# Projections spread over the attention chunks of an mLSTM layer, and the decay exponents in tiles of their own

## The chip, the cores and the metric

The kernel runs on one core of a Trainium2 chip. The metric is the device time of one execution in microseconds, median of several runs. The engines are named as in the profile: PE (TensorE, matrix products, with PEld its weight loads), DVE (VectorE), ACT (ScalarE), POOL (GpSimd) and SP, which issues the DMAs. Every engine runs its own queue in order and waits for the others at semaphores.

## The reference, cut to what matters

Two layers over 1024 latent and 256 context tokens of width 1024, in fp32. Layer 0 mixes with a short convolution, layer 1 with a bidirectional mLSTM; each is followed by a squared-ReLU MLP, which is most of the work. The change lies in the mLSTM mixer. Per direction, head and chunk of 128 tokens it computes

```python
b = jnp.cumsum(fc, axis=-1)
logd = b[..., :, None] - b[..., None, :] + ic[..., None, :]
logd = jnp.where(tri, logd, -jnp.inf)
inter = b + m[..., None]
m_t = jnp.maximum(inter, jnp.max(logd, axis=-1))
s = jnp.einsum('bhtd,bhsd->bhts', qc, kc) * jnp.exp(logd - m_t[..., None])
w_inter = jnp.exp(inter - m_t)
num = jnp.einsum('bhts,bhsv->bhtv', s, vc) + w_inter[..., None] * jnp.einsum('bhtd,bhdv->bhtv', qc, c_mat)
den = jnp.sum(s, axis=-1) + w_inter * jnp.einsum('bhtd,bhd->bht', qc, n_vec)
out = num / jnp.maximum(jnp.abs(den), jnp.exp(-m_t))[..., None]
...
c_new = a[..., None, None] * c_mat + jnp.einsum('bhsd,bhsv->bhdv', kc * wk[..., None], vc)
```

The outputs of both directions are added, normalized per head, multiplied with `sigmoid(o)` and projected with `w_out`. There are 8 heads with keys of 64 and values of 128.

## The kernel before, in words

**Precision.** A fp32 operand of a large product is split into a high and a low part in a PE format (`load_w`: DMA into `raw`, ACT casts the high part, DVE subtracts for the low part); a product then takes three passes. `raw` has three buffers, and the parts lie in a ring of eight slots, so that four weights are alive at a time. The small products of the attention are fp32 in one instruction, which shows as two records.

**The stage.** It works on head pairs j = 0 to 3. `Pair.k`, `.v` and `.q` project keys (three groups of tokens, `psk`), values (ten tiles, `psv`) and queries (two groups, `psq`) of a pair, each into one of the two PSUM tiles of the pool `tp`, from where ACT copies them to `kT`, `V` and `qz`. A gate stage on DVE and ACT (scans over all tokens, exponents) makes the rows of decays, of which `wkcol`, `acol` and `flcol` are transposes by PE (`ptg`), and the rows of maxima and of weights that go to DRAM (`nm_d`, `w_d`).

**States.** `states` goes through the ten chunks: PE transposes the keys (`pk`), DVE multiplies with the decays (`kk`), PE multiplies with the values, ACT and DVE copy the two directions into `sts`; then, for each head, eight dependent scans (L1004) accumulate the chunk states. One of the two directions runs backwards, so the second scan needs the last chunk.

**Attention.** `attend` takes one head, eight chunks. `front(c)`: for each two chunks a DMA broadcasts the rows of maxima to the tile `Dm` (two buffers); DVE adds the mask in place, ACT takes the exponent in place, PE computes keys by queries into `po` (pool `acc`, six PSUM tiles shared with `pk` and `pth`), and DVE multiplies both to `pm`. `back(c)`: four products with `V` and `sts` into the same `po`; ACT takes the absolute value of the denominators (`dn`), DVE maximum and reciprocal, ACT scales one direction (`h`), DVE adds the other (`hb`), ACT squares for the norm. `front` runs one chunk ahead of `back`.

**Gate and read-out.** `out_gate` normalizes `hb` (POOL computes `rstd`), projects the head's gate (two groups of 512, `pso`) and takes the sigmoid into `sg`; `read_out` transposes `hb` (`pth`) and multiplies. Heads 0 to 5 go to DRAM (`gd`), heads 6 and 7 stay in `sg` for the output projection (`op`).

**Order.** The program is written in the order: projections of pair j, gates and read-outs of pair j-1, states of pair j, attention of its two heads. The framework's scheduler then sets a fixed order for each engine at build time, by program order as priority and by what it thinks is ready; so parts of a later projection already stand between the products of the attention. The gates of the last three pairs are kept back to be mixed with the states and the attention of the last pair and to stand behind it.

Of the kernel before, what the change touches and what calls it, by code (L numbers as in the profile page):

```python
# [8 lines left out]
F32 = mybir.dt.float32  # L9
# [28 lines left out]
def hybrid_kernel(  # L38
# [769 lines left out]
    with ExitStack() as s1:  # L808
# [34 lines left out]
        class Pair:  # L843
# [12 lines left out]
            def k(self, groups, ps_pool=tp, tag="tp"):  # L856
                for t0, n in groups:
                    ps = ps_pool.tile([P, 512], F32, tag=tag, name="psk")
                    mm_feat(ps[:, 0:n], self.w, t0, n)
                    nc.scalar.copy(self.kT[:, t0 : t0 + n], ps[:, 0:n])  # L860

            def v(self, tiles):
                for t in tiles:
# [14 lines left out]
            def q(self, groups):  # L878
                w = load_w(wq[self.j])
                for t0, n in groups:  # L880
                    ps = tp.tile([P, 512], F32, tag="tp", name="psq")
                    mm_feat(ps[:, 0:n], w, t0, n)
# [4 lines left out]

        XG = ((256, 512), (768, 512))
        pair = Pair(0)
        pair.k(PG[0:2], acc, "acc")  # L890
        pair.v([0, 1, 2, 3, 4, 5, 7, 9])
        for f in pend:
            f(acc, "acc")
        pair.v([6, 8])
        gate_rows()
        pair.k(PG[2:])
        sT.close()
        with pool("gates", bufs=1, side="right") as gp:
# [60 lines left out]
            pair.q(XG)  # L959
            nxt = Pair(1)  # L960
            nxt.k(GROUPS)
# [18 lines left out]
        def states(pair):  # L980
            j = pair.j
            for c in range(NT):
# [9 lines left out]
                sb = 1 - c if c < NCT else NT + 1 - c  # L992
                for hh in range(2):
# [14 lines left out]
        def attend(pair, hh):  # L1008
            h = 2 * pair.j + hh
            kT, V, st = pair.kT, pair.V, sts[hh]  # L1010
            qw = hp.tile([P, SEQ], F32, tag="qw", name="qw")
            for d, r in enumerate((lower, upper)):
                nc.sync.dma_start(qw[r], w_d[d, h].partition_broadcast(64))
                nc.vector.tensor_mul(qw[r], qw[r], qz[hh * 64 : hh * 64 + 64, hh])
            if pair.j < HEADS // 2 - 1:
                hb = hp.tile([P, 8, P], F32, tag="hb", name="hb")
            else:
                hb = pr.tile([P, 8, P], F32, tag="V" if hh else "kT", name="hb")
            ssq = small.tile([P, 8], F32, tag="ssq", name="ssq", bufs=4)
            Dm = {}  # L1020

            def front(c):

                if c % 2 == 0:
                    D2 = hp.tile([P, 2, 2 * P], F32, tag="Dm", name="Dm")
                    nc.sync.dma_start(D2, nm_d[:, h, c * P : (c + 2) * P].partition_broadcast(P))
                    for d in range(2):
                        nc.vector.tensor_add(
                            ch(D2[:, d]), ch(D2[:, d]), mask[:, d].unsqueeze(1).broadcast_to([P, 2, P])
                        )  # L1030
                    Dm[c], Dm[c + 1] = D2[:, :, 0:P], D2[:, :, P : 2 * P]
                Dc = Dm[c]
                for d in range(2):
# [4 lines left out]
                    po[:, 0:P], kT[:, g * P : (g + 1) * P], qz[:, hh, c * P : (c + 1) * P], start=True, stop=True  # L1038
                )
                pm = hp.tile([P, 2, P], F32, tag="pm", name="pm")  # L1040
                nc.vector.tensor_mul(pm, po[:, 0:P].unsqueeze(1).broadcast_to([P, 2, P]), Dc)
                return po, pm

            def back(c, po, pm):
# [3 lines left out]
                for d in range(2):  # L1048
                    nc.tensor.matmul(o[:, d], pm[:, d], V[:, g, hh], start=True, stop=False)
                    nc.tensor.matmul(  # L1050
                        o[:, d], qw[:, c * P : (c + 1) * P], st[:, steps[d], d], start=False, stop=True
# [3 lines left out]
                nc.vector.tensor_max(dn, dn, flcol[:, c, :, h])  # L1055
# [3 lines left out]
                nc.vector.scalar_tensor_tensor(hb[:, c], o[:, 1, 0:P], dn[:, 1:2], h1, ALU.mult, ALU.add)  # L1059
# [155 lines left out]
```

## Time and profile before

| | us |
|---|---|
| median of three runs | 2564.34 (2563.26 to 2567.96) |
| the profiled execution, its own time | 2567.07 |
| its span, first to last instruction | 2565.3 |
| PE busy | 2485.2 (97%) |
| DVE busy | 1649.5 (64%) |
| ACT busy | 1141.6 (45%) |
| mLSTM stage, from the first key projection to the last read-out transpose | 1337.8 to 1809.2 |

The profile names an instruction by line, engine, operation and tile, and says of idle time which engine's instruction ended it. PE's clock has two levels, 1.2 and 2.4 GHz; the granted clock of a stretch is given as a share of the full one. Ends of matmuls are modelled, so starts are the safer reading.

### The profile page before, as it was taken

The page shows a single profiled execution, that of the slowest core. Times are in us where ns is not written, and L with a number is a line of the kernel's source. Part 1 is how long each engine was busy: PE and PEld are TensorE (multiplying, and loading weights), DVE is VectorE, ACT ScalarE, POOL GpSimd, SP SyncE. Part 2 cuts the span into 40 slices and gives each one's busy share as a digit, 9 for nine tenths or more (in the row PEclk, how much of TensorE's full clock was granted, in tenths as well). Part 3 has the DMA queues.
Part 4 walks back from the last instruction along what each step waited for, and adds up shares of the span by engine and source line. Part 5 has one row for each costly group of instructions (what it writes and reads, how often), then busy time and mean ns, then how long its engine had stood idle before and what let it go on. Part 6 is the DMA issues. An engine that isn't in the chain of part 4 may idle for free.

```text
span 2565.3 us, 38800 instructions
## 1 busy us (share of the span) xinstructions
PE 2485.2 (97%) x14520; PEld 2194.7 (86%) x14520; DVE 1649.5 (64%) x3058; ACT 1141.6 (45%) x2503; POOL 107.0 (4%) x229
## 2 busy tenths in 40 slices
PE   8999999999999999999999899999999999999998
PEld 6888887899999998888779788887789999988886
DVE  5777885687676654445864745537479788754565
ACT  6311112565445444334654434345456555544443
POOL 1000000100000000000121100000010000000010
PEclk9999999999999999999999899999999999999999
DMA  8456663436676675555751322222336788676665
GB/s 296 133 175 190 207 191 115 137 133 232 224 258 240 226 247 173 166 169 166 239 182 45 76 76 58 66 67 89 104 121 215 261 268 281 230 253 189 184 225 185
DMA packets 230207, 454.87 MB, mean 177 GB/s; under 512 B 17802, under 2 KB 109242, under 8 KB 230018
## 3 DMA queue, kind: packets, MB, share of 16 engines
q1 hardware_dynamic: 230018, 452.38, 54.5%
q8 instruction: 114, 1.87, 0.3%
q14 instruction: 75, 0.61, 0.1%
HBM read 326.78 MB, written 125.33 MB: 176 GB/s over the span
## 4 chain that ended last, share of the span: by engine, by line
PE 51%; issue 30%; DVE 7%; DMA 7%; ACT 3%; POOL 2%; DVEq 0%; SPq 0%; POOLq 0%; ACTq 0%
PE psd L538 11%; PE op L371 5%; PE psZ L433 4%; PE psW L433 4%; PE psX L433 4%; PE psv L867 3%; PE pso L129 3%; DMA Dm<-nm_d 3%; PE psc L129 3%; PE psb L129 2%; PE psu L129 2%; DMA mraw<-in_mod_w_dram 2%; PE psY L433 2%; PE psq L129 1%; DVE macc L220 1%
## 5 line engine op out<-in xcount | busy, mean ns | idle before, releaser
L538 PE MATMUL psd<-w,hp 128*128 128x512 f32 x3024 | 706.7, 395 | 0.6 <-DVE p L558 0.6
L538 PEld LDWEIGHTS psd<-w,hp 128*128 128x128 f32 x3024 | 568.1, 188 | 135.4 <-DVE p L558 1.5
L533 DVE TENSOR_TENSOR hp<-hr,hp 128x512 fp32r<-128x512 f32 (+1 forms) x226 | 169.0, 750 | 245.3 <-ACT hp L532 244.8
L123 DVE TENSOR_TENSOR w<-raw,w 128x512 fp32r<-128x512 f32 x394 | 267.6, 684 | 61.0 <-ACT w L122 60.6
L122 ACT CAST w<-raw 128x512 fp32r<-128x512 f32 x394 | 242.6, 618 | 119.4 <-DMA raw<-in_w_dram 43.1
L532 ACT CAST hp<-hr 128x512 fp32r<-128x512 f32 (+1 forms) x226 | 151.0, 669 | 312.6 <-PE psd L538 270.6
L433 PE MATMUL psX<-A,w 128*128 128x256 f32 (+1 forms) x1536 | 229.7, 297 | 2.9 <-ACT st L448 2.5
L433 PE MATMUL psZ<-A,w 128*128 128x256 f32 (+1 forms) x1536 | 227.7, 296 | 1.7 <-DVE st L452 1.6
L433 PE MATMUL psW<-A,w 128*128 128x256 f32 (+1 forms) x1536 | 227.1, 296 | 0.0
L433 PEld LDWEIGHTS psX<-A,w 128*128 128x128 f32 x1536 | 212.5, 188 | 4.7 <-ACT st L448 3.6
L433 PEld LDWEIGHTS psZ<-A,w 128*128 128x128 f32 x1536 | 212.2, 188 | 3.1 <-DVE st L452 2.8
L433 PEld LDWEIGHTS psW<-A,w 128*128 128x128 f32 x1536 | 212.1, 188 | 0.2 <-DVE st L454 0.2
L371 PE MATMUL op<-w,zs 128*128 128x512 f32 x864 | 206.1, 398 | 6.3 <-ACT zs L365 4.4
L371 PEld LDWEIGHTS op<-w,zs 128*128 128x128 f32 x864 | 162.8, 190 | 43.3 <-ACT zs L365 5.4
L463 ACT ACTIVATE st<-st 128x256 f32<-128x256 f32 (+1 forms) x192 | 85.1, 444 | 199.0 <-DVE st L454 132.8
L220 DVE SCALAR_TENSOR_TENSOR macc<-mraw,sil,macc 128x1024 f32<-128x1024 f32 x112 | 140.5, 1280 | 37.9 <-DMA mraw<-in_mod_w_dram 37.6
L109 ACT CAST w<-raw 128x1024 fp32r<-128x1024 f32 (+1 forms) x73 | 75.5, 1040 | 162.0 <-PE psc L129 60.0
L110 DVE TENSOR_TENSOR w<-raw,w 128x1024 fp32r<-128x1024 f32 (+1 forms) x73 | 87.6, 1209 | 80.1 <-ACT w L109 79.8
L867 PE MATMUL psv<-w,hT 128*128 128x256 f32 (+1 forms) x960 | 135.2, 295 | 0.5 <-ACT V L874 0.5
L867 PEld LDWEIGHTS psv<-w,hT 128*128 128x128 f32 x960 | 125.3, 194 | 1.1 <-ACT V L874 0.9
L433 PE MATMUL psY<-A,w 128*128 128x256 f32 (+1 forms) x768 | 116.6, 298 | 0.1
L129 PE MATMUL psc<-hT,w 128*128 128x512 f32 (+1 forms) x576 | 113.7, 348 | 0.5 <-DVE hT L279 0.4
(242 smaller groups left out, 3443.7 us busy)
## 6 DMA issues: line engine op xcount, KB each, us to landing
hid_d<-st SPq DMA_DIRECT2D x48, 896.0 KB, 5.0
mraw<-in_mod_w_dram SPq DMA_DIRECT2D x80, 512.0 KB, 4.1
raw<-in_w_dram SPq DMA_DIRECT2D x68, 512.0 KB, 4.2
hr<-hid_d SPq DMA_DIRECT2D x104, 320.0 KB, 3.4
rw<-in_w_dram SPq DMA_DIRECT2D x64, 512.0 KB, 6.0
raw<-t_d SPq DMA_DIRECT2D x128, 256.0 KB, 3.2
hr<-hid_d SPq DMA_DIRECT2D x122, 256.0 KB, 2.9
raw<-in_w_dram SPq DMA_DIRECT2D x96, 256.0 KB, 3.8
```

The costliest lines, as they stand in the source:

```text
L110: nc.vector.tensor_sub(w[1], src, w[0].bitcast(F32))
L122: nc.scalar.copy(w[:, 0], src)
L123: nc.vector.tensor_sub(w[:, 1], src, w[:, 0].bitcast(F32))
L129: nc.tensor.matmul(ps, w[a][:, k * P : (k + 1) * P], hold["hT"][:, k, b, t0 : t0 + n], start=(k == 0 and i == 0), stop=(k == KD - 1 and i ...
L220: nc.vector.scalar_tensor_tensor(ac[v], raw, s, ac[v], ALU.mult, ALU.add)
L371: nc.tensor.matmul(ps[h], zs[:, a, k, :], ws[k][b][:, h * 512 : (h + 1) * 512], start=(k == 0 and i == 0), stop=(k == KD - 1 and i == 2),)
L433: nc.tensor.matmul(ps, w[i][:, a, k * P : (k + 1) * P], A[:, PIECE[i], b, k, :], start=(first and k == 0 and j == 0), stop=(k == 3 and j = ...
L463: nc.scalar.activation(c, c, AF.Relu)
L532: nc.scalar.copy(h[:, 0], r)
L533: nc.vector.tensor_sub(h[:, 1], r, h[:, 0].bitcast(F32))
L538: nc.tensor.matmul(ps, h[:, a, o : o + P], w[:, b], start=(first and j == 0), stop=(last and j == 2))
L867: nc.tensor.matmul(ps[:, 0 : self.g], hold["hT"][:, k, a_, t * P : (t + 1) * P], self.wv[k // self.per][b_][:, k % self.per * self.g : (k ...
```

## The change

Three things, all in the mLSTM stage.

1. The projections return lists of units instead of running. A unit is one group of keys (256 or 512 tokens), one value tile, one group of queries, or half of the products of one 512-token group of a gate (`OutGate`, four units a head). `Spread` gives such a list out evenly over a number of steps. `states` calls it once a chunk (ten steps) and `attend`, which now takes both heads of a pair as one list of 16 chunks, once a chunk between `front(i+1)` and `back(i)`. In the states of pair j (from the second on) stand the gates and read-outs of pair j-1, in its attention the key, value and query projections of pair j+1. For the first pair three value tiles of the second stand in the states, the rest and the queries in the attention. In the last pair's attention stand head 5's gate and read-out, head 6's, and the first half of head 7's gate; the other half and head 7's read-out come behind it. Head 0's gate is projected in the gate stage.
2. The rows of maxima come for one chunk into a tile `row` (three buffers), fetched three chunks ahead; DVE's add of the mask writes `pm` (three buffers), in which the exponent and the product are then done in place. `Dm` is gone.
3. The multiplications of `qw` with the queries are done for both heads of a pair ahead of its attention; their transfers are issued ahead of the states.

```diff
+            def units(self):
+                if self.done:
+                    return []
+                self.done = True
+                return [lambda i=i: self.unit(i) for i in range(4)]
+
+            def unit(self, i):
+                if i == 0:
+                    self.w = load_w(wo[self.h])
+                    self.sg = sgp.tile([P, SEQ], F32, tag="sg", name="sg")
+                if i % 2 == 0:
+                    self.ps = tp.tile([P, 512], F32, tag="tp", name="pso")
...
+            def __call__(self):
+                self.i += 1
+                while self.done * self.steps < self.i * self.n and self.done < self.n:
+                    self.units[self.done]()
+                    self.done += 1
+
...
-            nxt.k(GROUPS)
+            run(nxt.k(GROUPS))
+            gates = [OutGate(h) for h in range(HEADS)]
+            run(gates[0].units())
             for src, dst, c0 in ((wkr, wkcol, 0), (a, acol, NCT), (m, flcol, NCT)):
...
+            def fetch(self, c):
+                row = hp.tile([P, 2, P], F32, tag="row", name="row", bufs=3)
+                nc.sync.dma_start(row, nm_d[:, self.h, c * P : (c + 1) * P].partition_broadcast(P))
+                self.rows[c] = row
+
+            def front(self, c):
+
+                h = self.h
+                Dc = hp.tile([P, 2, P], F32, tag="pm", name="pm", bufs=3)
+                nc.vector.tensor_add(Dc, self.rows[c], mask)
                 for d in range(2):
                     nc.scalar.activation(Dc[:, d], Dc[:, d], AF.Exp, bias=acol[:, c, d, h : h + 1])
...
+        def attend(pair, heads, step):
+            items = [(h, c) for h in heads for c in range(8)]
+            for h in heads:
+                h.begin()
+            nxt_ = heads[0].front(0)
+            for i, (hd, c) in enumerate(items):
+                cur = nxt_
+                if i + 3 < len(items):
+                    items[i + 3][0].fetch(items[i + 3][1])
+                if i + 1 < len(items):
+                    nxt_ = items[i + 1][0].front(items[i + 1][1])
+                step()
+                hd.back(c, *cur)
+
+        NPR = HEADS // 2
+        rest = lambda heads: [u for hd in heads for u in hd.out_gate() + [hd.read_out]]
+        heads, old = [], []
+        for j in range(NPR):
+            old = heads
             if j:
...
+            heads = [Head(pair, hh) for hh in range(2)]
+            for c in range(3):
+                heads[0].fetch(c)
+            if j == 0:
+                units = nxt.v(all_tiles) + nxt.q()
+                states(pair, Spread(units[0:3], NT))
+                units = units[3:]
+            else:
+                states(pair, Spread(rest(old if j < NPR - 1 else old[0:1]), NT))
+                if j < NPR - 1:
+                    nxt = Pair(j + 1)
+                    units = nxt.k(GROUPS) + nxt.v(all_tiles) + nxt.q()
+            last = []
+            if j == NPR - 1:
+                last = heads[1].out_gate()
+                units = rest(old[1:2]) + rest(heads[0:1]) + last[0:2]
+            attend(pair, heads, Spread(units, 16))
+        run(last[2:])
+        heads[1].read_out()
```

The built order of the instructions shows three of the places.

DVE at the end of the gate stage, before: the last row of the gate rows, the low halves of the weights of the second pair's queries (`w_13707`) and head 0's gate (`w_13772`), the transposed decays, then the first pair's states (`kk`, `st`).

```order
L952 TENSOR_SCALAR M__12747<-M__12747 40x1280
L110 TENSOR_TENSOR w_13707<-raw,w_13706 128x1024
L970 COPY wkcol<-ptg 128x10x8 x2
L970 COPY acol<-ptg 128x8x8 x2
L970 COPY flcol<-ptg 128x8x8 x2
L110 TENSOR_TENSOR w_13772<-raw,w_13771 128x1024
L987 TENSOR_TENSOR kk<-pk,wkcol 128x128 x4
L1000 COPY st_12978<-pk 64x129 x2
```

The same place after; `w_12942` is the low half of head 0's gate weight, `w_13720` that of the second pair's queries.

```order
L1008 TENSOR_SCALAR M__12747<-M__12747 40x1280
L110 TENSOR_TENSOR w_12942<-raw,w_12941 128x1024
L110 TENSOR_TENSOR w_13720<-raw,w_13719 128x1024
L1028 COPY wkcol<-ptg 128x10x8 x2
L1028 COPY acol<-ptg 128x8x8 x2
L1028 COPY flcol<-ptg 128x8x8 x2
L1045 TENSOR_TENSOR kk<-pk,wkcol 128x128 x2
L110 TENSOR_TENSOR w_14084<-raw,w_14083 128x1024
L1078 TENSOR_TENSOR qw<-qw,qz 64x1024
```

The gate's weight is now wanted by PE ahead of the transposes, and its subtraction stands where the queries' stood, behind the last of the gate rows; a multiplication of `qw` has come between the first `kk`.

DVE in the attention of the second pair, before: the add of the mask to two chunks of `Dm`, and the rest of three chunks mixed with the normalization of the head before (`hb<-hb,rstd`).

```order
L1028 TENSOR_TENSOR Dm<-Dm,mask 128x256 x2
L1059 SCALAR_TENSOR_TENSOR hb<-po,dn,h_14264 128x128
L1055 TENSOR_TENSOR dn<-dn,flcol 128x2
L1072 TENSOR_TENSOR hb<-hb,rstd 128x512
L1056 RECIPROCAL dn<-dn 128x2
L1041 TENSOR_TENSOR pm<-po,Dm 128x256
```

After, one chunk of the same pair; this row of five repeats, chunk by chunk.

```order
L1094 TENSOR_TENSOR pm<-row,mask 128x256
L1117 TENSOR_TENSOR dn<-dn,flcol 128x2
L1103 TENSOR_TENSOR pm<-po,pm 128x256
L1118 RECIPROCAL dn<-dn 128x2
L1121 SCALAR_TENSOR_TENSOR hb<-po,dn,h_14292 128x128
```

The add no longer comes in twos on a tile that holds two chunks' exponents, but once a chunk, from a tile that nothing else uses.

ACT in the attention of the last pair, before: a sigmoid of a gate among the exponents, with a load of the function table ahead of it and one behind.

```order
L1080 ACT_TABLE_LOAD
L1080 ACTIVATE sg<-pso 128x512
L1058 ACTIVATE h_16107<-po,dn 128x128
L1054 ACTIVATE dn<-po 128x2 x2
L1034 ACT_TABLE_LOAD
L1034 ACTIVATE Dm<-Dm,acol 128x128
```

After, one of five such places in that attention.

```order
L1122 ACTIVATE h_16234,ssq<-hb 128x128
L930 ACT_TABLE_LOAD
L930 ACTIVATE sg<-pso 128x512
L1116 ACTIVATE dn<-po 128x2
L1096 ACT_TABLE_LOAD
L1096 ACTIVATE pm<-pm,acol 128x128
L1120 ACTIVATE h_16268<-po,dn 128x128
```

The shape of the place is the same; what has moved is how often it comes, as three gates of the last pair's time now lie in its attention at even distances.

## Rows read from the trace of the kernel before

**Rows 1.** The page's engines: busy us (share of the span), instructions.

```profile
PE 2485.2 (97%) x14520; PEld 2194.7 (86%) x14520; DVE 1649.5 (64%) x3058; ACT 1141.6 (45%) x2503; POOL 107.0 (4%) x229
```

**Rows 2.** PE's waits, 1380 to 1900 us: for whom, us, times, longest.

```profile
PE po L1037 <- DVE hb L1059: 14.1, 11, 2.1
PE po L1049 <- DVE pm L1041: 8.0, 5, 3.0
PE ptg L965 <- ACT l L947: 4.7, 1, 4.7
PE op L371 <- ACT zs L365: 2.7, 1, 2.7
PE pth L1087 <- DVE hb L1059: 2.1, 1, 2.1
PE op L371 <- DVE zs L366: 1.9, 1, 1.9
PE po L1037 <- DVE dn L1055: 1.8, 1, 1.8
```

**Rows 3.** Windows: length, busy PE, PEld, DVE, ACT, POOL (instructions), PE clock, DMA.

```profile
1555.00:1588.00 33.00, 26.65 (x212) 25.00 (x212) 18.49 (x69) 21.98 (x95) 2.90 (x5) 1.00 0.40 98
1588.00:1640.00 52.00, 52.00 (x302) 45.51 (x302) 12.30 (x12) 12.37 (x20) 0.93 (x1) 1.00 0.17 51
```

**Rows 4.** Windows of 10 us, first and last of five below full clock.

```profile
1460.00:1470.00 10.00, 7.43 (x47) 6.89 (x45) 4.33 (x17) 5.01 (x22) 1.22 (x2) 0.83 0.53 109
...
1680.00:1690.00 10.00, 7.76 (x63) 7.35 (x62) 6.37 (x25) 6.33 (x29) 1.73 (x2) 0.97 0.41 120
```

**Rows 5.** DVE's timeline (start, us, operation, idle before); tile `Dm`: releasers, landing.

```profile
1674.53 0.76 DVE L1028 TENSOR_TENSOR Dm<-Dm,mask 128x256 f32<-128x256 f32 x2 [2.44 <-DMA Dm<-nm_d]
...
  DMA Dm<-nm_d: 39.0, 22
...
DMA to landing us min/median/max: 5.2/5.2/5.2
```

**Rows 6.** PE's timeline: values, two chunk products, gate projections.

```profile
1587.80 17.36 PE L867 MATMUL psv<-w,hT 128*128 128x256 f32 x144 [0.20 <-ACT V L874]
...
1670.08 0.39 PE L1050 MATMUL po<-st,qw 128*128 128x129 f32 x2
1670.31 0.39 PE L1049 MATMUL po<-V,pm 128*128 128x129 f32 x2
...
1785.30 22.19 PE L129 MATMUL pso<-hT,w 128*128 128x512 f32 x94
```

**Rows 7.** Timeline of all engines at the end of the gate stage.

```profile
1418.26 0.56 ACT L860 COPY kT<-psk 128x512 f32<-128x512 f32 x1
...
1418.40 1.29 PE L965 MATMUL ptg<-ident,l 40*128 40x40 f32 x10 [4.66 <-ACT l L947]
1418.42 1.21 DVE L110 TENSOR_TENSOR w<-raw,w 128x1024 fp32r<-128x1024 f32 x1
```

**Rows 8.** DVE's timeline at the end of the second pair's states.

```profile
1546.38 4.86 DVE L1004 SCALAR_TENSOR_TENSOR st<-st,adb 128x258 f32<-128x258 f32 x12
```

**Rows 9.** ACT's table loads: groups (count, busy us, mean ns); timeline of one.

```profile
L1080 ACT ACT_TABLE_LOAD x6 | 7.7, 1283 | 0.1
...
L1034 ACT ACT_TABLE_LOAD x5 | 6.4, 1283 | 2.8 <-DMA Dm<-nm_d 2.7
...
1757.83 1.28 ACT L1034 ACT_TABLE_LOAD   x1
1759.12 0.40 ACT L1034 ACTIVATE Dm<-Dm,acol 128x128 f32<-128x128 f32 x1
```

**Rows 10.** Timelines of PE and DVE at the end of the first pair.

```profile
1484.81 0.64 PE L1050 MATMUL po<-st,qw 128*128 128x129 f32 x2
...
1489.71 1.29 DVE L1072 TENSOR_TENSOR hb<-hb,rstd 128x512 f32<-128x512 f32 x2 [0.86 <-POOL rstd L242]
```

More of the change, by code (lines that the diff above doesn't have):

```diff
@@ L856, in k, with unit @@
             def k(self, groups, ps_pool=tp, tag="tp"):
-                for t0, n in groups:
+                def unit(t0, n):
                     ps = ps_pool.tile([P, 512], F32, tag=tag, name="psk")
@@ L860, in k, with unit @@
                     nc.scalar.copy(self.kT[:, t0 : t0 + n], ps[:, 0:n])
+                return [lambda g=g: unit(*g) for g in groups]
             def v(self, tiles):
-                for t in tiles:
+                def unit(t):
                     ps = tp.tile([P, 512], F32, tag="tp", name="psv")
@@ L958, in hybrid_kernel @@
             ring["n"] += 2
-            pair.q(XG)
+            run(pair.q())
             nxt = Pair(1)
-            nxt.k(GROUPS)
+            run(nxt.k(GROUPS))
+            gates = [OutGate(h) for h in range(HEADS)]
+            run(gates[0].units())
             for src, dst, c0 in ((wkr, wkcol, 0), (a, acol, NCT), (m, flcol, NCT)):
@@ L978, in hybrid_kernel, with states @@
             nc.gpsimd.memset(t[lower, :, 1], 0.0)
-        def states(pair):
+        def states(pair, step):
             j = pair.j
@@ L1006, in states @@
                     )
[L1008 to L1032, printed above, removed]
@@ new lines, in hybrid_kernel, with __init__, begin @@
+        class Head:
+            def __init__(self, pair, hh):
+                self.pair, self.hh, self.h = pair, hh, 2 * pair.j + hh
+                self.qw = hp.tile([P, SEQ], F32, tag="qw", name="qw")
+                for d, r in enumerate((lower, upper)):
+                    nc.sync.dma_start(self.qw[r], w_d[d, self.h].partition_broadcast(64))
+                self.rows, self.gate = {}, gates[self.h]
+            def begin(self):
+                pair, hh = self.pair, self.hh
+                for r in (lower, upper):
+                    nc.vector.tensor_mul(self.qw[r], self.qw[r], qz[hh * 64 : hh * 64 + 64, hh])
+                if pair.j < HEADS // 2 - 1:
+                    self.hb = hp.tile([P, 8, P], F32, tag="hb", name="hb")
+                else:
+                    self.hb = pr.tile([P, 8, P], F32, tag="V" if hh else "kT", name="hb")
+                self.ssq = small.tile([P, 8], F32, tag="ssq", name="ssq", bufs=4)
+            def fetch(self, c):
[6 more added lines that the diff above has]
+                nc.vector.tensor_add(Dc, self.rows[c], mask)
```

106 lines of the change are left out of this document (52 added, 54 removed).

## The prediction, before the changed kernel ran

> **What bounds the kernel now.** I read the page's engine table first: TensorE (PE) is busy 97% of the span [rows 1]. So time can only be won where PE stands still or runs at its half clock, and the change touches only the mLSTM stage, some 1380 to 1810 us. Next the waits of PE in that stage [rows 2]: 26.0 us are in the attention of the four head pairs (14.1 + 8.0 + 2.1 + 1.8, behind `hb`, `pm`, `hb` again and `dn`), 4.7 us behind the gate rows, 4.6 us where the output projection starts. The windows [rows 3] say why the first group can go: in 1555 to 1588, attention of the second pair, PE is busy 26.65 of 33 us and ACT 21.98; in the 52 us behind it, where the rest of the value, the query and the gate projections run, PE is full and DVE and ACT do 12 us each. The work that could fill the holes stands directly behind them. Then the clock [rows 4]: in five slices of 10 us it is under 1, from 0.83 in 1460 to 1470 to 0.97 in 1680 to 1690, each at or behind a PE wait (0.83, 0.83, 0.66, 0.86, 0.97). A slice at clock c loses 10(1 - c) us; the five lose 8.5 us, of which some 1.6 lie inside the 3 us wait that is counted already. So 6.9 us.
>
> What makes PE wait is DVE's queue [rows 5]. The add of the mask is done in place on `Dm`, which holds two chunks and has two buffers; its refill can only be issued when both chunks' products are done, takes 5.2 us to land, and DVE then stands 2.4 us at a time, 39.0 us in 22 waits, with `hb` and `pm` of the chunks before queued behind.
>
> **What goes.** The rows of maxima get a tile of their own, freed by the add itself, one chunk each, three buffers, fetched three chunks ahead; the exponent lies in `pm`. A fetch has three chunks' time instead of less than one transfer. A unit of value projection is 24 of the 144 matmuls in 17.36 us, 2.9 us; a 512-wide unit is 24 of 94 in 22.19, 5.7 us, a gate unit half of that; a chunk's own five fp32 products are 1.1 us, from two starts 0.22 us apart [rows 6]. So a chunk takes 4.0 us or more in pairs two and three, some 2.55 us in the first (two chunks to a unit), about 2.5 to 3.2 in the last. Three chunks are 7.5 to 12 us against 5.2 us for a transfer that is now half as large. I take the DMA wait at zero. And with a unit ahead of each chunk PE has other work while ACT and DVE go through exp, product, maximum, reciprocal. PE's matmuls are the same in number and shape. Removed: 26.0 + 6.9 = 32.9 us, if nothing takes their place.
>
> **What is added**, term by term:
> - The gate stage. Gate 0's projection is put between the keys and the transposes `ptg`. It doesn't cover the 4.7 us wait: its PSUM tile is freed by the copy of keys that ACT runs behind the exponent, at 1418.26 + 0.56, and its third pass wants the low half of the weight, which DVE's order puts behind the whole chain, 1418.42 + 1.21 [rows 7]. PE starts at 1419.6 instead of 1418.4: **+1.2 us** (0 to 2.5). The 11.3 us of gate work are moved, not added; behind them on PE wait `ptg` and with it DVE's `wkcol`, so DVE begins its part of the states later.
> - The scans. Behind the last `pk` of a pair DVE has a copy and 13 more scans, 4.86 us for 12 [rows 8], together some 5.6 us, before the products that read the last state. In the first pair of before 40 value matmuls, 4.8 us, stand there, and PE did not wait. In the changed order I count 15 value matmuls and six products in the first pair, 3.1 us, 20 wide matmuls and three products in the second, 5.3, 17 narrow and 11 wide ones and four products in the third, 5.4, 17 wide ones and four products in the last, 4.8: short by 2.5 + 0.3 + 0.2 + 0.8 = 3.8 us; with some half clock behind the first gap **+4.5 us** (0 to 8).
> - The first pair's states. Two more multiplications of `qw` come ahead of the scans on DVE, each about as long as a subtraction of as many columns, 1.21 us [rows 7], while of PE's value matmuls only 120 stand there (14.4 us) to hide them. Between none of it on the path and all of it with a wait for each of the two, **+2 us** (0 to 4).
> - The first pair's chunks at 2.55 us: nearest is the attention of the second pair in before, 33 us for 14 chunks with its DMA waits [rows 3], 2.36 us. Just enough; **+1.5 us** (0 to 4).
> - The last pair. Its 16 chunks get 12 gate units, and each 512 columns end in a sigmoid among exponents. ACT loads its function table 21 times in the stage instead of 11 (6 + 5), 1283 ns each [rows 9]: 12.8 us more in all, hidden in pairs one to three, where ACT has room. In the last pair's attention: 16 chunks at 1.57 us (21.98 us for 14, [rows 3]) 25.1, ten loads 12.8, five sigmoids, each taken as a copy of 512 columns, 0.56 [rows 7], 2.8, together 40.7 us, against PE's 91 gate matmuls 21.4 and 16 chunks 17.8, together 39.2, and 16 transposes. PE and ACT are level; the slack of a chunk decides. Before, in its last pair, PE waited 1.8 us, behind `dn`, at such a sigmoid [rows 2]. **+4 us** (0 to 9, five times 1.8).
> - The end. Before, 94 gate matmuls hide the last head's normalization; now 24 do, 5.7 us. The nearest rows are the end of the first pair: from the start of its last product, 1484.81, to the end of the first half of the multiplication that waits for POOL, 1489.71 + 0.65, are 5.5 us, part of it at the half clock [rows 10]. It just fits. The waits of the output projection behind it, 2.7 and 1.9 us [rows 2], stay: the same multiplications, casts and subtractions stand ahead of its first operand. **0** (-1.5 to +1.5).
> - SP's queue. 64 row fetches in place of 32 `Dm`, issued between weight loads and stores of `gd`, which wait for DVE. A fetch stands behind such a wait by at most one chunk by the order: **0**, and the rival below.
>
> Sum: 32.9 - (1.2 + 4.5 + 2 + 1.5 + 4) = 32.9 - 13.2 = 19.7 us. Against the profiled execution, whose own time is 2567.07, that is 2547.4; it lies 2.7 over the median of the runs, 2564.34, so I forecast **2545 us**.
>
> One rule speaks against the change. On ACT a load is followed at once by the exponent, 1757.83 + 1.28 and next start 1759.12 [rows 9]: a switch costs 1.29 us here. The Trainium skill, ScalarE: Activation LUTs, section What ACT_TABLE_LOAD costs, gives 1283 ns for the load and about 1380 ns of drain beside it, 2.66 us a switch, and its section on table sets asks to do all calls of one set together. The load agrees with the row; the drain is not in this trace. By the page the ten loads of the last pair would take an estimate of 13.8 us more, and the sum would be 2559.
>
> **Rivals.**
> (a) *The wait moves to the scans and the states.* For it: PE's order is now tied to the chunks, and the scans can't start before the last `pk`. Against: in pairs two to four keys and gates of 4 to 5 us are still pulled in ahead of them. Both terms at their upper ends and the gap's half clock: 2545 + 3.5 + 2 + 2.5 + 2 = 2555.
> (b) *ACT bounds the last pair.* All ten loads on the path in place of 4 us: 2545 + 8.8 = 2554. For it: 40.7 against 39.2. Against: three `pm` and six PSUM tiles let PE run ahead by a chunk or two.
> By the price in the Trainium skill, ScalarE: Activation LUTs, the same mechanism would end at 2559; no drain shows in the rows, so that price gets no chance beside (b)'s own.
> (c) *Nothing takes their place*, each added term at its lower end: 2564.3 - 32.9 = 2531.
> (d) *Slower: the row fetches come late.* SP issues in order, and rows stand behind weight loads that wait for DVE. It decides where SP is held longer than three chunks less the transfer: 7.7 - 5.2 = 2.5 us in the first pair, 9 - 5.2 = 3.8 in the last. Then each of these 32 fetches is exposed as the 32 of `Dm` were (39.0 us on DVE, 26.0 on PE, 6.9 of clock): 2545 + 32.9 = 2578. For it: three buffers of raw weights serve all loads, so SP does wait for DVE's subtractions. Against: by the changed order such a load waits for a subtraction that stands three adds or more ahead of the row behind it.
>
> **How the numbers follow.** Forecast 2545 with 0.62; (a) 0.13, (b) 0.10, (c) 0.08, (d) 0.07. The range: the low end is (c), 2531, less a microsecond of holes too short to be listed; the high end takes all added terms at their upper bounds, 2.5 + 8 + 4 + 4 + 9 + 1.5 = 29, 2564.3 - 3.9 = 2560. It leaves out (d) and a tail of (a) and (b). Within 0.2%, about what a measurement of this kernel can tell from no change, is 2559.2 to 2569.5: faster has 0.85 (the forecast but 0.03, most of (a) and (b), (c)), same 0.08, slower 0.07.
>
> **What would show it.** Right: no wait of DVE for the rows' DMA; no PE wait behind `hb` in pairs two and three; clock 1.00 from 1500 to 1780; a PE wait before the first gate projection of about 6 us; one gap of 1 to 3 us behind the last `pk` of a pair; short gaps by sigmoids in the last pair. Wrong: `row` among DVE's releasers (d); PE waits for `st` of several us (a); for `pm` behind ACT's loads (b). The forecast falls if fetches or order give PE new holes in pairs two and three, for which the trace of before has no row.

## The result, and the profile after

The changed kernel takes **2526.4 us** (median of 4 runs, 2524.4 to 2528.7) against 2563.8 us of the kernel before beside it: ratio 0.985, 95% interval 0.9835 to 0.987. A second group of runs gave 2527.2 against 2561.6, ratio 0.987 (0.985 to 0.988). Every group ran the kernel before beside its own kernels, so ratios compare across groups better than times do. The forecast was 2545 with a range of 2530 to 2560: faster, as said, but by 37 us and not by 19, and below the range.

The engines' busy time in the page after:

```profile
PE 2465.9 (98%) x14520; PEld 2180.4 (86%) x14520; DVE 1650.6 (65%) x3058; ACT 1158.4 (46%) x2513; POOL 108.2 (4%) x229
```

The same 14520 matmuls keep PE busy for 19.3 us less than in [rows 1]. Where that comes from is seen in the mLSTM stage. The next two rows are windows from the first wait in the projection of keys to the first matmul of the output projection, of before and of after (length, busy PE, PEld, DVE, ACT, POOL with instructions, PE clock, DMA share, GB/s):

```profile
1339.86:1811.89 472.03, 437.85 (x2800) 392.48 (x2801) 253.01 (x664) 207.69 (x638) 32.55 (x44) 0.97 0.26 72
```

```profile
1337.58:1773.92 436.34, 422.15 (x2801) 381.01 (x2801) 255.76 (x665) 224.87 (x648) 33.58 (x44) 1.00 0.30 78
```

The stage is 35.7 us shorter. PE's idle time falls from 34.2 to 14.2 us, by 20.0, and its *busy* time for the same matmuls falls from 437.9 to 422.2, by 15.7. The second number matters for what follows: busy time isn't work.

PE's waits from 1380 to 1900, after (who waited for whom: total, times, longest):

```profile
PE pso L922 <- ACT kT L860: 5.6, 1, 5.6
PE op L371 <- ACT zs L365: 3.5, 1, 3.5
...
PE pk L1054 <- DVE st L1059: 3.2, 3, 1.5
PE po L1111 <- DVE pm L1103: 1.5, 1, 1.5
PE op L371 <- DVE zs L366: 1.1, 1, 1.1
PE pk L1054 <- DVE kk L1045: 0.2, 1, 0.2
```

Of the four groups in the attention in [rows 2], 26.0 us, one wait of 1.5 us is left, in the first pair. New are 3.4 us of `pk`, in the states of pairs two to four. VectorE's waits for the rows, 1380 to 1800, tell why: it now waits for PE to free a `pm` tile, with its rows already there, and only once for a transfer.

```profile
DVE pm L1094 <- PE po L1111: 67.2, 28, 5.0
DVE pm L1094 <- DMA row<-nm_d: 2.5, 1, 2.5
```

The second row answers to 39.0 us in 22 waits in [rows 5]. The clock in 10 us windows, after; the last answers to [rows 4], and the first is the only one under 1 from 1340 to 1770:

```profile
1410.00:1420.00 10.00, 4.42 (x14) 3.10 (x13) 7.98 (x14) 7.94 (x9) 1.34 (x2) 0.83 0.11 14
...
1460.00:1470.00 10.00, 8.52 (x73) 8.29 (x73) 7.11 (x31) 7.14 (x36) 0.00 (x0) 1.00 0.22 47
```

### The profile page after: what moved, and what is told of

It is laid out like the page before. It is cut to its first block, busy times and chain, and to the rows that moved or that the text cites. A ratio compares the mean times of both kernels' runs of the same rounds, so it can differ in the third digit from the quotient of the medians.

```text
span 2523.4 us, 38819 instructions
## 1 busy us (share of the span) xinstructions
PE 2465.9 (98%) x14520; PEld 2180.4 (86%) x14520; DVE 1650.6 (65%) x3058; ACT 1158.4 (46%) x2513; POOL 108.2 (4%) x229
## 4 chain that ended last, share of the span: by engine, by line
PE 52%; issue 30%; DVE 7%; DMA 5%; ACT 3%; POOL 2%; DVEq 0%; SPq 0%; POOLq 0%; ACTq 0%
PE psd L538 12%; PE op L371 5%; PE psv L869 4%; PE psZ L433 4%; PE psW L433 4%; PE psX L433 4%; DMA mraw<-in_mod_w_dram 3%; PE pso L922 3%; PE psc L129 2%; PE psu L129 2%; PE psY L433 2%; PE psb L129 2%; DVE macc L220 1%; PE psq L129 1%; PE psk L129 1%
## 5 line engine op out<-in xcount | busy, mean ns | idle before, releaser
L869 PE MATMUL psv<-w,hT 128*128 128x256 f32 (+1 forms) x960 | 130.1, 289 | 0.0
L129 PE MATMUL psu<-hT,w 128*128 128x512 f32 (+1 forms) x576 | 112.4, 347 | 0.0
```

The costliest lines, as they stand in the source:

```text
L129: nc.tensor.matmul(ps, w[a][:, k * P : (k + 1) * P], hold["hT"][:, k, b, t0 : t0 + n], start=(k == 0 and i == 0), stop=(k == KD - 1 and i ...
L869: nc.tensor.matmul(ps[:, 0 : self.g], hold["hT"][:, k, a_, t * P : (t + 1) * P], self.wv[k // self.per][b_][:, k % self.per * self.g : (k ...
```

## The experiments

Two questions were open. Which part of the change wins the time: the rows fetched ahead (theory 1, the prediction's: the refill of `Dm` makes PE wait) or the projections between the chunks (theory 2: PE lacks other work)? And why were the added terms, 13.2 us in the forecast, so much smaller?

### One part of the change at a time

**The rows alone**, in the kernel before:

```diff
-                if c % 2 == 0:
-                    D2 = hp.tile([P, 2, 2 * P], F32, tag="Dm", name="Dm")
-                    nc.sync.dma_start(D2, nm_d[:, h, c * P : (c + 2) * P].partition_broadcast(P))
...
+                Dc = hp.tile([P, 2, P], F32, tag="pm", name="pm", bufs=3)
+                nc.vector.tensor_add(Dc, rows[h, c], mask)
...
+                if 8 * hh + c + 3 < 16:
+                    fetch(pair.j, 8 * hh + c + 3)
```

> The kernel before with one part of the change alone: rows of maxima in a tile of one chunk with three buffers, fetched three chunks ahead, and the exponents in the tile of the product; the projections stay where they were. Theory 1, the prediction's: the refill of Dm is the cause of TensorE's waits in the attention (26.0 us and 6.9 us of half clock), so most of both go without any spreading: 2564 - (20 to 33) = 2531 to 2544. Theory 2: what is missing is other work for TensorE between the steps of a chunk; with the DMA wait gone, the chain exponent, product, maximum, reciprocal still takes ScalarE and VectorE longer than the five products (1.1 us) of a chunk, so TensorE goes on waiting behind hb and pm, only shorter: 2564 - (5 to 12) = 2552 to 2559. Both expect no wait of VectorE for the rows.

**The spreading alone**: the changed kernel with `Dm` as before; the early gate and the multiplications of `qw` stay as changed.

```diff
-                Dc = hp.tile([P, 2, P], F32, tag="pm", name="pm", bufs=3)
-                nc.vector.tensor_add(Dc, self.rows[c], mask)
+                if c % 2 == 0:
+                    D2 = hp.tile([P, 2, 2 * P], F32, tag="Dm", name="Dm")
+                    nc.sync.dma_start(D2, nm_d[:, h, c * P : (c + 2) * P].partition_broadcast(P))
...
```

> The changed kernel with the rows of maxima as before: Dm of two chunks, two buffers, the mask added in place, products in a tile of their own. Theory 1: a refill of Dm is issued when two chunks' products are done and is wanted two chunks later; that is 8 us in the second and third pair, enough for 5.2 us of landing, but 5.1 us in the first pair and 5 to 6.4 in the last, so there VectorE waits again by 1 to 2 us for each of 8 refills a pair, and TensorE with it: 2526 + (6 to 20) = 2532 to 2546. Theory 2: with a unit of projection ahead of each chunk TensorE doesn't see such a wait in any pair: 2526 plus 0 to 3. Both expect waits of VectorE for Dm.

Measured: the rows alone 2547.0 us (ratio 0.9945, 0.993 to 0.996, beside 2561.8 of before), the spreading alone 2554.0 (0.997, 0.9956 to 0.998). One part is worth 14.8 us and the other 7.8, together 22.6, and both at once 34 to 37. Neither number lies in the range of either theory. Nor is either run one part and nothing else, for the scheduler sets a new order after each edit: by the traces some 320 of the 2804 matmul records of the stage stand elsewhere with the rows alone than in the kernel before, and some 150 with the spreading alone than in the changed kernel. The traces say what happened. The kernel with the rows alone, PE's waits from 1380 to 1900, then VectorE's for the rows:

```profile
PE po L1047 <- DVE pm L1039: 6.3, 6, 1.7
PE ptg L965 <- ACT l L947: 4.8, 1, 4.8
PE po L1036 <- DVE dn L1053: 2.9, 2, 1.9
...
PE po L1047 <- ACT pm L1033: 1.9, 2, 1.2
PE po L1047 <- ACT dn L1052: 1.8, 2, 1.1
...
PE po L1036 <- DVE hb L1057: 1.2, 1, 1.2
PE po L1047 <- DVE dn L1054: 0.6, 2, 0.4
```

```profile
DVE pm L1031 <- DMA row<-nm_d: 20.5, 17, 2.3
```

In the attention 14.7 us are left of 26.0, and VectorE still waits 17 times for rows, though they are fetched three chunks ahead. Half the bytes don't land in half the time: issues by transfer (KB each, median us from issue to landing), before and with the rows alone:

```profile
Dm<-nm_d SPq DMA_DIRECT2D x32, 256.0 KB, 5.2
```

```profile
row<-nm_d SPq DMA_DIRECT2D x64, 128.0 KB, 4.6
```

Where no projection stands between the chunks, a chunk is short. Three score products in a row from PE's timeline of that kernel, second pair (start, us):

```profile
1547.40 0.39 PE L1036 MATMUL po<-qz,kT 128*128 128x128 f32 x2
...
1548.85 0.39 PE L1036 MATMUL po<-qz,kT 128*128 128x128 f32 x2
...
1549.97 0.39 PE L1036 MATMUL po<-qz,kT 128*128 128x128 f32 x2
```

At 1.1 to 1.5 us a chunk, three chunks are 3.4 to 4.4 us, and the row takes 4.6. With the spreading alone the wait for `Dm` stays, and gets worse; VectorE's waits there, and two rows from its and PE's timelines at the end of the first pair (start, us, operation, idle before):

```profile
DVE Dm L1092 <- DMA Dm<-nm_d: 67.1, 26, 5.3
```

```profile
1506.26 0.76 DVE L1092 TENSOR_TENSOR Dm<-Dm,mask 128x256 f32<-128x256 f32 x2 [4.34 <-DMA Dm<-nm_d]
...
1511.06 0.80 PE L1054 MATMUL pk<-V,kk 128*128 128x129 f32 x2 [7.70 <-DVE kk L1045]
```

VectorE stands 4.3 us for `Dm`; behind that add is queued the product of the next pair's keys with the decays (`kk`), and PE waits 7.7 us for it. Between the two VectorE stands another 1.9 us for a weight whose cast, on ScalarE, is queued behind the exponents of the same `Dm`. A projection ahead of each chunk doesn't help there: the wait holds VectorE's queue, and with it work that has nothing to do with the rows.

### Is it the landing of the rows?

Three kernels take the rows-alone kernel further: a second chunk in flight, one fetch a pair and no other, and a fourth buffer.

```diff
-            nxt_ = front(0)
+            ahead = [front(0), front(1)]
...
+                if c < 6:
+                    ahead.append(front(c + 2))
+                back(c, *ahead[c])
```

> The kernel before with the rows of maxima apart, as in the run of that part alone (2547.0), and besides with exponents and score products of two chunks ahead of the chunk that is read out in place of one (four buffers for them; the first half of the sum is written where the sum goes). If what TensorE still waits for there is the length of the chain exponent, product, maximum, reciprocal of one chunk, a second chunk in flight covers it: 14.7 us of waits and 2.6 of half clock go for the most part, 2547 - (9 to 16) = 2531 to 2538. If it is the throughput of ScalarE or VectorE, or the landing of the rows (VectorE waits 20.5 us for them there), another chunk ahead changes little: 2543 to 2549.

Measured: 2546.2 us, no change (2547.0; the intervals 0.992 to 0.995 and 0.993 to 0.996 overlap). A longer lead of the exponents and scores is worth nothing while the rows come as late as before: VectorE waits 19.1 us for them here and 20.5 there. Whether the chain through ScalarE and VectorE in one chunk would hold PE if the rows were there is seen in the next run.

```diff
+            if i:
+                rows[h, c] = rows[2 * j, 0]
+                return
             rows[h, c] = hp.tile([P, 2, P], F32, tag="row", name="row", bufs=3)
```

> The kernel before with the rows apart (2547.0), but with one fetch of rows a pair, whose tile serves all 16 chunks, so that no chunk waits for a transfer; the maxima of the other chunks are left out, so the output isn't the reference's. If what is left of the waits there (14.7 us on TensorE, 20.5 us of VectorE behind the rows) comes from the landing of the rows, 4.6 us against three chunks of 1.5 us where no projection stands between them: 2547 - (8 to 16) = 2531 to 2539. If it comes from the place of the projections (taken up in bunches, the chunks between them bare, and bare chunks bound by the way through ScalarE and VectorE): 2542 to 2547.

Measured: **2529.1 us** (0.9875, 0.986 to 0.989), 18 us under the rows alone, and lower than the whole range of the first theory. Its stage window and PE's waits, 1380 to 1900:

```profile
1342.97:1777.34 434.37, 424.78 (x2800) 384.12 (x2800) 249.65 (x664) 204.21 (x638) 32.50 (x44) 0.99 0.20 60
```

```profile
PE ptg L965 <- ACT l L947: 5.0, 1, 5.0
...
PE op L371 <- ACT zs L365: 2.7, 1, 2.7
PE pk L995 <- DVE st L1000: 1.9, 1, 1.9
PE op L371 <- DVE zs L366: 1.3, 1, 1.3
```

This is the order of the rows-alone kernel but for some two dozen of the 2804 matmul records, with nothing spread, and PE waits nowhere in the attention: the chain of one chunk isn't what was left. The stage, 434.4 us, is even 2 us shorter than that of the changed kernel, though the whole kernel isn't. So the place of the projections, as the scheduler mixes them in with the rows apart, was good enough; the fetches were the whole of what was left. But taking 60 fetches away also takes their load off the queue. How much of it is lead is told by the fourth buffer:

```diff
-            rows[h, c] = hp.tile([P, 2, P], F32, tag="row", name="row", bufs=3)
+            rows[h, c] = hp.tile([P, 2, P], F32, tag="row", name="row", bufs=4)
...
-                if 8 * hh + c + 3 < 16:
-                    fetch(pair.j, 8 * hh + c + 3)
+                if 8 * hh + c + 4 < 16:
+                    fetch(pair.j, 8 * hh + c + 4)
```

> The kernel before with the rows apart (2547.0), fetched four chunks ahead into four buffers instead of three (the room comes from writing the first half of the sum where the sum goes); everything is computed. With one fetch a pair the time was 2529, so the fetches cost 18 us there. If that is their way (4.6 us from issue to landing against three chunks of some 1.5 us), a fourth buffer gives 1.5 us more and takes most of VectorE's 20.5 us behind the rows: 2547 - (9 to 16) = 2531 to 2538. If it is the load of 64 fetches on the queue or on the transfers beside them, a fourth buffer changes nothing: 2545 to 2548.

Measured: 2538.5 us (0.990, 0.988 to 0.992), 8.5 us under the rows alone, half a microsecond short of the range, with as many fetches as the rows-alone kernel. (It writes the first half of the sum in place; so does the kernel with a second chunk in flight, which gained nothing.) Its waits:

```profile
DVE pm L1031 <- DMA row<-nm_d: 3.2, 7, 0.9
```

```profile
PE po L1036 <- DVE hb L1057: 3.8, 3, 1.6
...
PE po L1047 <- DVE pm L1039: 1.5, 2, 0.9
PE po L1036 <- DVE dn L1053: 1.5, 2, 0.8
```

VectorE's 20.5 us for rows fall to 3.2 and PE's 14.7 to 6.8. So the lead of a fetch, which is chunks times the length of a chunk, against 4.6 us of landing, is shown as the cause of 8.5 of the 18 us. Both parts of the change lengthen the lead: the separate tile makes it three chunks, and with the spreading a chunk takes 2.9 us in the mean of the first and last pairs and 4.3 in the others, from score product to score product, where the rows-alone kernel has 1.9 to 2.3. That fits their being worth more together than apart. The other 9 us between this kernel and the one with a single fetch weren't settled. The stage holds 6.1 of them (440.5 against 434.4 us), about the 6.8 us of PE's waits that are left; a lead that is still short in the shortest chunks, the load of the fetches, and an order in which some 150 matmul records stand elsewhere are all possible.

### The added terms

**The last pair's sigmoids**, left out:

```diff
-                    nc.scalar.activation(self.sg[:, t0 - CTX : t0 - CTX + 512], self.ps, AF.Sigmoid)
+                    nc.scalar.activation(self.sg[:, t0 - CTX : t0 - CTX + 512], self.ps, AF.Identity if self.h > 4 else AF.Sigmoid)
```

> The changed kernel with the sigmoids of the last three heads left out (a copy in their place), so that ScalarE loads no function table among the exponents of the last pair; the output isn't the reference's. The prediction's term for that pair (ScalarE level with TensorE, +4 us with a range of 0 to 9): 2526.4 - 4 = 2522. Theory now, by the profile after, which shows no wait of TensorE in the last pair: the loads lie beside TensorE's work whole, so 2526 +- 1.5.

Measured: 2526.4 us against 2527.2 of the changed kernel beside it (0.9869 and 0.9866), no difference. The loads of function tables among ScalarE's groups in the stage (count, busy us, mean ns), first of the changed kernel, then without the sigmoids:

```profile
L930 ACT ACT_TABLE_LOAD x11 | 14.1, 1283 | 0.2
L1096 ACT ACT_TABLE_LOAD x10 | 12.8, 1283 | 0.2
```

```profile
L930 ACT ACT_TABLE_LOAD x6 | 7.7, 1283 | 0.1
L1096 ACT ACT_TABLE_LOAD x6 | 7.7, 1283 | 0.1
```

Nine loads less, 11.5 us of ScalarE, and not one microsecond of time. The window of the last pair's attention in the changed kernel says why:

```profile
1722.00:1764.00 42.00, 42.00 (x266) 37.06 (x264) 27.82 (x90) 36.10 (x101) 1.83 (x2) 1.00 0.40 103
```

ScalarE is busy 36.1 of 42 us and PE 42.0: ScalarE is close, but not late. The Trainium skill, ScalarE: Activation LUTs, section What ACT_TABLE_LOAD costs, adds some 1380 ns of drain to a load of 1283 ns; for nine loads that would be an estimated 12 us more, beyond the 5.9 that ScalarE has free in this window. The trace doesn't agree: behind each of the nine loads in the window the next sigmoid or exponent starts 0.01 us later, and PE waits for nothing.

**The last pair's gate pieces, behind its attention** as before:

```diff
-                units = rest(old[1:2]) + rest(heads[0:1]) + last[0:2]
+                units, tail = [], rest(old[1:2]) + rest(heads[0:1]) + last
...
-        run(last[2:])
+        run(tail)
```

> The changed kernel with the gate pieces of the last pair's attention written behind it, as before, so that only what the order of the program pulls forward lies between the chunks; the rows stay apart, and the other pairs stay as changed. If even spreading is what closes the holes, the last pair loses it: waits behind pm, hb and dn as in the kernel with the rows alone, some 4 to 6 us and 2 of half clock, less the 0 to 1 us that the end may win: 2527 + (4 to 8) = 2531 to 2535. Rival: with the rows apart the order that the kernel before had serves as well: 2527 +- 1.5.

Measured: 2531.7 us (0.988, 0.9865 to 0.9895), 4.5 to 5.3 us above the changed kernel, near the low end of what even spreading was said to be worth. The two were timed in different groups, and the intervals overlap; in the profiles the stage is 440.5 us long against 436.3 and 435.9, which bears out the sign. Two waits behind `dn`, 2.2 us, come back, PE is busy 39.8 of 42 us, and VectorE waits three times for rows, 3.7 us, instead of once:

```profile
PE po L1099 <- DVE dn L1117: 2.2, 2, 1.6
```

```profile
1728.00:1770.00 42.00, 39.76 (x246) 34.24 (x246) 28.85 (x96) 28.14 (x99) 3.67 (x4) 1.00 0.36 107
```

**The first gate's place**, first without the early projection, then with it and its causes of waiting removed:

```diff
-            run(gates[0].units())
```

> The changed kernel without the first gate's projection ahead of the transposes of the gate rows; it joins the other gate in the states of the second pair. The prediction's step says that its place costs 1.2 us of waiting, so 2526.4 - 1.2 = 2525.2. Rival: it pays, since the profile after shows 1.7 us of half clock in the gate stage where there were 3.4 before, and since more of it lies ahead of the scans of the first pair than it costs: wait 4.7 us in place of 5.6, half clock 3.4 in place of 1.7, in all 2526.4 - 0.9 + 1.7 = 2527 or more.

```diff
-                    self.w = load_w(wo[self.h])
+                    with tc.high_priority(offset=0 if self.h else HP):
+                        self.w = load_w(wo[self.h])
...
-                    self.ps = tp.tile([P, 512], F32, tag="tp", name="pso")
+                    pl, tag = (tp, "tp") if self.h else (acc, "acc")
+                    self.ps = pl.tile([P, 512], F32, tag=tag, name="pso")
```

> The changed kernel with the first gate's projection accumulated in a PSUM tile of the other pool (six tiles, which no copy of keys has to free) and its weight's halves split ahead of the scans of the gate rows. If the 5.6 us wait ahead of it comes from these two alone (the tile behind ScalarE's copy of keys, the low half behind VectorE's chain), TensorE goes through from the keys to the gate without a gap: the projection then ends some 11.3 us after 1411.5, at 1422.8, later than the last exponent of the gate rows, about 1417.8, so the transposes don't wait either: 2526.4 - 5.6 - 1.7 (half clock) = 2519, by this 2518 to 2521. Rival: the subtraction put ahead of the scans makes the gate rows later by 1.2 us and the wait only moves to the transposes or to the first pair's states: 2524 to 2527.

Measured: without it 2529.2 us (0.988, 0.986 to 0.990), on the rival's side, though the intervals overlap; its stage is 437.8 us long against 436.3 and 435.9. The wait is 4.8 us there instead of 5.6, but the transposes and states behind it run at a mean clock of 0.71 in 1420 to 1430. With tile and weight free 2519.9 us. The rows of the wait in the changed kernel, all engines:

```profile
1416.45 0.56 ACT L860 COPY kT<-psk 128x512 f32<-128x512 f32 x1
1416.61 1.21 DVE L110 TENSOR_TENSOR w<-raw,w 128x1024 fp32r<-128x1024 f32 x1
...
1417.06 12.72 PE L922 MATMUL pso<-hT,w 128*128 128x512 f32 x48 [5.58 <-ACT kT L860]
```

ScalarE's copy of keys stood in its queue behind an exponent that waited 11.1 us for VectorE; and VectorE's split of the weight came last in its chain. Both causes were removed at once; what each is worth alone wasn't tried. The kernel ran again beside the changed one, since the first time stood in another group:

> The kernel with the first gate's projection in the other PSUM pool and its weight split early, once more, beside the changed kernel on the same chip. If the 5.6 us wait and 1.7 us of half clock are all that it takes away: 6 to 7 us under the changed kernel. If the first result (2519.9 against 2526.4 of another group) held a difference of the chips: 3 us under it or less.

> The changed kernel as it is, so that the others of this group have it beside them on the same chip: 2526 +- 2.

Measured: 2520.7 against 2527.2 us, 6.5 us less (0.984, 0.983 to 0.986, against before), as the first reading said. PE's timeline there:

```profile
1403.73 9.72 PE L129 MATMUL psk<-hT,w 128*128 128x512 f32 x41
1413.29 11.37 PE L924 MATMUL pso<-hT,w 128*128 128x512 f32 x48
...
1424.59 0.81 PE L1025 MATMUL ptg<-ident,l 40*128 40x40 f32 x10
```

Keys, gate and transposes follow each other without a gap, no window of the gate stage is under full clock, and the 48 matmuls of the gate take 11.37 us instead of 12.72. This kernel beats both.

**The end**, in that kernel: a gate piece between the halves of the last read-out.

```diff
-        run(last[2:])
-        heads[1].read_out()
+        run(last[1:3])
+        heads[1].read_out(last[3])
```

> The kernel with the first gate's early projection (2520.7), with one gate piece fewer in the last pair's attention and the last head's read-out in two halves, a gate piece of 2.9 us between them, so that TensorE has work while the first half of the last head becomes the first operand of the output projection. If the 4.6 us wait there is the way of that operand through VectorE and ScalarE: 2520.7 - 2.9 = 2518. Rival: ScalarE's cast of the output projection's weights waits for the last gate's weight to come free, which is 2.9 us later, and the wait stays: 2520 to 2522.

Measured: 2519.9 us (0.9836 against 0.9842), between the two and no difference that these runs can tell; the trace speaks for the rival. The wait for the first operand is still 3.97 us, and that operand stands in ScalarE's queue behind casts of weights, the first of which waits 4.68 us until the gate's last matmul frees the buffer that it writes.

```profile
1763.39 1.05 ACT L109 CAST w<-raw 128x1024 fp32r<-128x1024 f32 x1 [4.68 <-PE pso L924]
...
1768.00 4.47 PE L371 MATMUL op<-w,zs 128*128 128x512 f32 x9 [3.97 <-ACT zs L365]
```

## Why the forecast was too small a gain

**The mechanism was right, and two sizes failed**: what goes was put at 32.9 us and was 40.0, and the added terms, 13.2 in the sum, were 4.1. `Dm`'s refill made PE wait: with the rows apart and one fetch a pair, 26.0 us of waits and all half clock of the attention go with nothing spread, though in an order that isn't quite that of before. The step "I take the DMA wait at zero" held for the changed kernel (2.5 us, once, and the 1.5 us of PE behind it), and rightly rested on the length of the chunks: without spreading it fails (20.5 us).

**The removed side was too small by 7.1 us, and one view hid it.** The forecast took 26.0 of waits and 6.9 of half clock. It saw five slices under full clock; the stage has seven, and the two from 1410 to 1430 (0.89 and 0.77) lose 3.4 us more. Measured, PE's busy time for the same matmuls fell by 15.7 us: the 6.9, another 1.7 in the gate stage (those 3.4 us before, 1.7 in one slice after), and 7.1 that remain, which no list of waits and no clock row shows. I worked a window with its busy share, 26.65 of 33 us in [rows 3]; but its 112 records of single products, 97 value matmuls and three key matmuls, at the 0.22 us from start to start of [rows 6] for each two, 17.36 / 144 and 22.19 / 94 each, come to 12.3 + 11.7 + 0.6 = 24.6 us. (I also took the window for 14 chunks; on PE it holds the products of 12.) The missing 2.0 us lie about the waits: the two records of a product show 0.39 us, with an end that the profile models, when nothing follows, and 0.22 when something does. Four pairs of up to 2.0 can hold the 7.1; that is an estimate. Where the waits go it goes: 437.9 us busy before, 424.8 with one fetch a pair (some of that at a clock of 0.52, in the gate stage from 1420 to 1430), 420.6 in the kernel with the free gate tile, which has hardly any half clock either.

**The added side was too large by 9.1 us**: 4.1 measured, 13.2 forecast.

| term | forecast | measured |
|---|---|---|
| gate stage | +1.2 | -0.8: wait +0.9, half clock -1.7 |
| scans | +4.5 | 0, no wait behind the last `pk` |
| first pair's states | +2 | 0 there; 2.5 of the last line are the same work in pairs three and four |
| first pair's chunks | +1.5 | +1.5, but behind one late row, so the number fits by luck |
| last pair | +4 | 0, by the run without sigmoids too |
| end | 0 | 0: 4.6 us, as in [rows 2] |
| not foreseen | | +3.4, `pk` in the states |

The term for the gate stage had the wait right (5.6, I said 5.9), but left out what the projection behind the wait does for the clock: the work at half clock is now the gate's, PE enters the transposes and the states at full speed, and taking the projection away makes the stage 1.4 to 1.9 us longer.

The term for the scans failed in the count of PE's work. VectorE has a copy and 13 scans behind the last `pk` of the first pair, as I said. But up to the product at 1459.71, which starts when the eleventh of these scans is done, I had put 15 value matmuls and six products on PE, 3.1 us; the trace has 24 and ten there, 5.1 us, and no wait. The scans on VectorE and that product on PE:

```profile
1455.06 4.87 DVE L1063 SCALAR_TENSOR_TENSOR st<-st,adb 128x258 f32<-128x258 f32 x12
...
1459.71 0.39 PE L1112 MATMUL po<-st,qw 128*128 128x129 f32 x2
```

The last pair was a tie by my sum, 40.7 against 39.2; in the window ScalarE is busy 36.1 of 42 us, and even a tie isn't yet a wait. That three `pm` tiles in flight took up the rest is likely, but wasn't tested.

The `pk` waits are three, 0.7 to 1.5 us. The longer two, 2.5 us in pairs three and four, stand behind the multiplications of `qw`, which the change puts ahead of the attention and so among the states' copies in VectorE's queue; I had priced them for the first pair alone. Before the longest, the multiplication itself waits for its transfer:

```profile
1702.49 1.22 DVE L1078 TENSOR_TENSOR qw<-qw,qz 64x1024 f32<-64x1024 f32 x1 [1.57 <-DMA qw<-w_d]
...
1704.30 0.49 PE L1054 MATMUL pk<-V,kk 128*128 128x129 f32 x2 [1.47 <-DVE st L1059]
```

The third, in pair two, comes from the read-out of the pair before, whose multiplication by `rstd` VectorE now does between the copies.

Together 32.9 + 7.1 - 4.1 = 35.9 us, against 35.7 measured in the stage (the gate stage's clock is in the 4.1); as the 7.1 is a remainder, the sum had to close. The spans of the two profiled executions differ by 41.9 us: another 2.3 lie ahead of the stage and 3.9 behind it, where nothing was changed. The medians differ by 37.4.

**The rivals.** (a) and (b) didn't come: no wait for scans, none behind table loads. (c), nothing takes the waits' place, 2531, was nearest, and still 5 us too high, for the hidden part. (d), late rows, shows once, in the first pair; in the kernels with bare chunks rows come late too, there where three chunks are short, a condition that (d) didn't name. The range was built from the upper ends of costs; its low end took (c) and one microsecond for "holes too short to be listed", which were 7.

## What to carry to other kernels

A fetch's lead is a number of buffers times the time of a step; compare it with the landing time for the shortest step there is, and remember that every stall that is removed shortens the step. Work put between steps can then be worth its time as lead for a transfer, not only as cover for an engine. To see what a stretch can give, take the matmuls in it at their back-to-back rate, not the engine's busy share, which counts the tail of each lone instruction as work. And look for a ready copy that stands in a queue behind something that waits: 6.5 us lay there and in a weight that was split late.

## What the hardware showed

Landing time followed the size only weakly here. Issues by transfer in the changed kernel (KB each, median us from issue to landing):

```profile
raw<-in_w_dram SPq DMA_DIRECT2D x96, 256.0 KB, 3.6
...
row<-nm_d SPq DMA_DIRECT2D x64, 128.0 KB, 4.8
```

A row read by all 128 partitions takes 4.8 us (4.6 in the rows-alone kernel) for 128 KB and took 5.2 for 256 KB: by an estimate from these, 4.0 to 4.4 us of it don't depend on the size. A plain load of 256 KB is faster, 3.6 us. The Trainium skill, DMA: Bandwidth & Descriptors, section Anatomy of one DMA, fits another path by 2.0 us and 436 GB/s, an estimate of 2.3 us for 128 KB; the rows here take twice that.

A load of a function table costs ScalarE 1283 ns each time, and cost PE nothing in the last pair, where ScalarE had that time free. And the clock that falls in a wait stays down into the work behind it: the gate's 48 matmuls take 12.72 us behind a 5.6 us wait (13.17 in the second profile, behind 5.2) and 11.37 without one, so a wait there costs 1.4 to 1.8 us more than its length.
